# Attention's value products for two heads at once, in two 64-column tiles of TensorE's array

## The chip, the cores and the metric

One core of one Trainium2 chip runs the whole program. The metric is the device time of one execution in microseconds (us); the time of a kernel is the median over its runs. Engines are called as the profile calls them: PE (TensorE's matrix products), PEld (its weight loads), DVE (VectorE), ACT (ScalarE), POOL (GpSimd) and SP (SyncE, here a queue that issues DMAs).

## The reference, cut to what matters

The model has two layers, a Fourier layer and an attention layer, on 256 tokens and 256 context tokens. The change is in the attention of layer two: 64 query heads of width 64 share 8 heads of keys and values, and the softmax has one more term, the sink.

```python
s = jnp.einsum('bqhgd,bkhd->bhgqk', q, k).astype(jnp.float32) * (ATTN_HEAD_DIM ** -0.5)
if mask is not None:
    s = jnp.where(mask, s, NEG_INF)
sk = jnp.broadcast_to(sink..., s.shape[:-1] + (1,))
p = jax.nn.softmax(jnp.concatenate([s, sk], axis=-1), axis=-1)[..., :-1]
return jnp.einsum('bhgqk,bkhd->bqhgd', p.astype(v.dtype), v)      # the value products
...
y = jnp.moveaxis(o, 0, 1).reshape(b, n, D_BRANCH) * jax.nn.silu(z)
```

The last line shows what follows: the 64 x 64 = 4096 columns of attention output are multiplied by a gate computed from z, another product of the input with weights, and go through the output projection.

## The kernel before, in words

**Precision.** Operands are split in two parts, high and low, and a product is a sum of products of parts. Large products use three (high x high, high x low, low x high): that is `mm3`, lines 145 to 147, which nearly every group of the profile carries. For the value products both operands are f16 parts. The values v of a block of 128 keys are one tile `va` of 128 x 8 x 128: for each of the 8 value heads 64 columns of high parts and, beside them, 64 columns of low parts (lines 1248 to 1255; `v01[kb]` for the four blocks kb of 128 keys).

**The attention stage** is the loop over i from 0 to 65 (line 1550). Round i computes the scores and the softmax of head i (`stage_s`), and the value products of head i - 2 (`stage_o`), so that the work between lies two rounds apart. Between them stand two calls of `filler()`, each of which emits one unit of the large products of this layer from a fixed list (line 1379): q for the next heads, z for the blocks, and at the end the first part of the output projection. These units are what PE does while a head's softmax goes through DVE, ACT and a DMA. The order of the instructions on each engine is fixed when the program is built: a scheduler sorts what the loop emits by estimated readiness.

**One head's chain.** PE forms the scores of two blocks of 128 queries (lines 1483, 1484); DVE adds the mask and finds the maximum (1485); ACT takes the exponential (1488); DVE and ACT form the reciprocal of the sum; ACT and DVE write the normalised probabilities as a high and a low f16 half, `f` (1500, 1501); two DMAs on SP's queue transpose them into `ft`, keys on the partitions (1503). For heads 61 to 63 PE does the transposing (`stage_t`, lines 1506 to 1511). `ft` holds 8 x 2 x 128 columns: index j is 0 to 3 for the high parts of the four key blocks and 4 to 7 for the low parts. `ft` has 3 buffers.

**The value products before** (`stage_o`, line 1513). For each of the four key blocks two matmuls: the stationary operand is all 128 columns of `va` (64 high, 64 low), the moving operand is 256 queries of `ft`, once the high and once the low part. So 8 matmuls of 128x256 fill one PSUM tile `oo`, whose upper 64 rows hold the products with v's high part and the lower 64 rows those with its low part. ACT copies the lower half out (`ot`, 1524) and DVE adds it to the upper (`ob`, 1525); the head with odd number fills the lower half of `ob`. When both heads of a block are there, `emit_y` (1460) multiplies `ob` by the scale and by the gate `th`, if the unit of z for this block is done; else the unit of z calls it.

**PSUM.** All products share one pool of 8 banks (`psum()`, line 44).

**Another place that uses part of the array.** Early in the kernel `ada_tile` (line 279) has a stationary operand of only 32 columns. It writes four products into the four 32-row parts of one PSUM bank, `oa[0][j * 32 : (j + 1) * 32]`, which puts each of them in another 32-column tile of the array (line 286). The prediction uses its rows.

Of the kernel before, what the change touches and what calls it, by code (L numbers as in the profile page):

```python
# [10 lines left out]
F32 = mybir.dt.float32  # L11
F32R = mybir.dt.float32r
F16 = mybir.dt.float16
AF = mybir.ActivationFunctionType
ALU = mybir.AluOpType
AX = mybir.AxisListType

P = 128
# [4 lines left out]
N = 256  # L23
# [9 lines left out]
def tile_dit(ctx: ExitStack, tc: tile.TileContext, a: dict, out: bass.AP):  # L33
    nc = tc.nc
    V, S, PE, GP = nc.vector, nc.scalar, nc.tensor, nc.gpsimd
# [8 lines left out]
    def psum():  # L44
        return pp.tile([P, 512], F32, tag="ps", name="ps")
# [593 lines left out]
    for g in range(G):  # L639
        for j in {13: (8, 9), 14: (10, 11)}.get(g, (g - 5,) if 5 <= g < 13 else ()):  # L640
            t = up.tile([P, 1024], F32, name="pz", tag="pz", bufs=1)
# [217 lines left out]
    with tc.tile_pool(name="yp", reuse_waits="tile", bufs=32) as ypool:  # L859
# [171 lines left out]
        for i in range(32):  # L1031
# [26 lines left out]
            if kg >= 12:  # L1058
                for k in range(sw * 8 + (kg - 12) * 2, sw * 8 + (kg - 12) * 2 + 2):
                    t = act()  # L1060
# [79 lines left out]
    with tc.tile_pool(name="h1", reuse_waits="tile", bufs=16) as h1p:  # L1140
# [119 lines left out]
        with tc.tile_pool(name="at", reuse_waits="tile", bufs=2) as at:  # L1260
# [209 lines left out]
            def stage_s(i):  # L1470
                hk, blk, hh = i // 8, i // 2, i % 2
                p2, pr = (blk % 4) // 2, blk % 2
                kkh, kkl = kk[hk]
                q2 = qq[hk, p2][hh]
                pt = [at.tile([P, 512], F32, tag="p", name="p", bufs=3) for _ in range(2)]
                mx = at.tile([P, 2], F32, tag="mx", name="mx")
                sm = at.tile([P, 2], F32, tag="sm", name="sm")
                es = at.tile([P, 2], F32, tag="es", name="es")
                so = []
                for tb in range(2):  # L1480
                    o = psum()
                    st = q2[:, (pr * 2 + tb) * P : (pr * 2 + tb + 1) * P]
                    PE.matmul(o, st, kkh, start=True, stop=False)  # L1483
                    PE.matmul(o, st, kkl, start=False, stop=True)  # L1484
                    V.tensor_tensor_reduce(o, o, mask[:, tb, :], -0.125, nsink[:, i : i + 1], ALU.add, ALU.min, mx[:, tb : tb + 1])  # L1485
                    so.append(o)
                for tb in range(2):
                    S.activation(pt[tb], so[tb], AF.Exp, bias=mx[:, tb : tb + 1], scale=-1.0, accum_out=sm[:, tb : tb + 1])  # L1488
                S.activation(es, mx, AF.Exp, bias=sink[:, i : i + 1])
                V.scalar_tensor_tensor(sm, sm, 1.0 / PS, es, op0=ALU.mult, op1=ALU.add)  # L1490
                V.reciprocal(sm, sm)
                ft = at.tile([P, 8, 2, P], F16, tag="ft", name="ft", bufs=3)
                fs = []
                for tb in range(2):
                    if i < 61:
                        f = at.tile([P, 1024], F16, tag="f", name="f", bufs=3)
                    else:
                        f = actp.tile([P, 1024], F16, tag="act", name="f")
                        fs.append(f)
                    fa = S.activation(f[:, 0:512], pt[tb], AF.Copy, scale=sm[:, tb : tb + 1]).ins  # L1500
                    f_last[:] = fa, V.scalar_tensor_tensor(f[:, 512:1024], pt[tb], sm[:, tb : tb + 1], f[:, 0:512], op0=ALU.mult, op1=ALU.subtract).ins  # L1501
                    if i < 61:
                        nc.sync.dma_start_transpose(ft[:, :, tb, :], f)
                return ft, fs
# [5 lines left out]
                        PE.transpose(o[:, j, :], fs[tb][:, j * P : (j + 1) * P], ident16[0])  # L1510
                    (S.copy if tb == 0 else V.tensor_copy)(ft[:, :, tb, :], o)

            def stage_o(i, ft, fs):
                hk, blk, hh = i // 8, i // 2, i % 2
                oo = psum()
                for kb in range(4):
                    fh, fl = (ft[:, j, :, :].rearrange("p t q -> p (t q)") for j in (kb, 4 + kb))
                    PE.matmul(oo[:, 0:N], v01[kb][:, hk, :], fh, start=kb == 0, stop=False)  # L1518
                    PE.matmul(oo[:, 0:N], v01[kb][:, hk, :], fl, start=False, stop=kb == 3)  # L1519
                if hh == 0:  # L1520
                    obs[blk, 0] = at.tile([P, N], F32, tag="ob", name="ob", bufs=4)
                ob = obs[blk, 0]
                t = at.tile([64, N], F32, tag="ot", name="ot", bufs=1)
                S.copy(t, oo[64:128, 0:N])
                V.tensor_tensor(ob[hh * 64 : hh * 64 + 64, :], oo[0:64, 0:N], t, op=ALU.add)
                if hh == 1:
                    obs[blk, 1] = ob
                    emit_y(blk)

            first = 10  # L1530
            for i in range(first):
# [18 lines left out]
            for i in range(66):  # L1550
                if i % 8 == 0:
                    while defer:
                        defer.pop(0)[1]()
                if i == 61:
                    t = actp.tile([P, 1024], F16, tag="act", name="ident16")
                    ident16.append(t[:, 0:P])
                    S.copy(ident16[0], ident)
                y_sums(12, i if i < 60 else 99)
                if i == 62:
                    out_scale()  # L1560
                if i < 64:
                    pts[i] = stage_s(i)
                if i - 2 >= 61:
                    stage_t(*pts[i - 2])
                filler()
                if i >= 2:
                    stage_o(i - 2, *pts.pop(i - 2))
                filler()


# [244 lines left out]
```

## Time and profile before

| | us |
|---|---|
| median of 3 runs | 1761.97 |
| lowest and highest run | 1761.92, 1764.43 |
| span of the profiled execution, first to last instruction | 1759.3 |
| median less span, taken as what lies around the span | 2.67 |
| attention loop's value products, first and last start | 1139.2, 1617.5 |
| PE busy / DVE busy / ACT busy in the span | 1726.3 / 1404.7 / 1141.0 |

The page has no time of the profiled execution other than its span, so the difference to the median stands for the rest. A row of the timeline gives the start, the duration, the engine, the line, the operation, what it writes and reads, the array's part in use (128*128 is all of it, 128*32 is 32 of its columns), the shape and the number of merged instructions. A matmul's duration includes the way through the array, so matmuls that follow each other overlap in the list: what a matmul costs PE is the distance to the next start, not its duration. In brackets stands the idle time before an instruction and what ended it.

### The profile page before, as it was taken

The numbers are of one execution on the slowest core, as the hardware profiler recorded it, in microseconds if no ns is written. First come the engines' busy times: TensorE is split into PE (matmuls) and PEld (weight loads), VectorE is DVE, ScalarE is ACT, GpSimd is POOL, SyncE is SP. The second block draws the span as 40 slices with busy tenths as digits, with TensorE's granted clock in tenths as the row PEclk, the third lists the DMA queues.
The fourth block names the chain that finished last, engine by engine and source line by source line (L and its number), as shares of the span: only waits on it lengthen the run. The fifth ranks groups of instructions, "written<-read, shape, count | busy, mean of one in ns | idle before, by whom it ended". The sixth has DMA issues, their size and how long they took to land.

```text
span 1759.3 us, 27829 instructions
## 1 busy us (share of the span) xinstructions
PE 1726.3 (98%) x10051; PEld 1173.5 (67%) x10051; DVE 1404.7 (80%) x2443; ACT 1141.0 (65%) x2165; POOL 355.5 (20%) x485
## 2 busy tenths in 40 slices
PE   6999999999999999999999999999999999999997
PEld 4679999644444444446444745789889888987464
DVE  5779889797676786877689685989998889988755
ACT  5545556486777755465235496678888788888643
POOL 0002111211222104212310221412303221251001
PEclk9999999999999999999999999999999999999999
DMA  9998999778998969977997594588878888878643
GB/s 393 417 357 254 277 270 262 286 286 305 337 314 297 315 228 371 382 250 258 391 330 234 193 364 163 186 198 209 222 209 193 213 216 210 215 182 289 223 169 120
DMA packets 232298, 465.72 MB, mean 265 GB/s; under 512 B 154496, under 2 KB 154896, under 8 KB 205280
## 3 DMA queue, kind: packets, MB, share of 16 engines
q1 hardware_dynamic: 180672, 331.41, 57.4%
q0 software_dynamic: 47344, 125.58, 22.4%
q10 hardware_dynamic: 4144, 6.95, 1.1%
q8 instruction: 79, 1.29, 0.3%
q14 instruction: 59, 0.48, 0.1%
HBM read 419.30 MB, written 12.59 MB: 245 GB/s over the span
## 4 chain that ended last, share of the span: by engine, by line
PE 91%; DVE 3%; DMA 3%; ACT 2%; issue 1%; POOL 0%; ACTq 0%; POOLq 0%; SPq 0%; DVEq 0%
PE ps L145 27%; PE ps L146 27%; PE ps L147 27%; DMA raw<-in_awp 2%; PE ps L1518 2%; PE ps L1483 2%; PE ps L1484 2%; PE ps L1519 2%; PE ps L286 1%; ACT wf L137 1%; DMA ft<-f 0%; ACT act L877 0%; PE ps L1370 0%; DVE wf L138 0%; DVE act L984 0%
## 5 line engine op out<-in xcount | busy, mean ns | idle before, releaser
L67 DVE TENSOR_TENSOR wl<-raw,wh 128x1024 fp32r<-128x1024 f32 x152 | 200.2, 1321 | 44.3 <-ACT wh L66 30.6
L66 ACT CAST wh<-raw 128x1024 fp32r<-128x1024 f32 x152 | 158.7, 1045 | 62.9 <-PE ps L146 42.1
L146 PE MATMUL ps<-act,wf 128*128 128x512 f16 x512 | 194.0, 379 | 0.0
L147 PE MATMUL ps<-act,wf 128*128 128x512 f16 x512 | 191.1, 379 | 0.0
L145 PE MATMUL ps<-act,wf 128*128 128x512 f16 x512 | 189.8, 379 | 0.6 <-ACT wf L137 0.3
L145 PE MATMUL ps<-y,wf 128*128 128x512 f16 x448 | 169.8, 379 | 0.8 <-ACT wf L137 0.8
L146 PE MATMUL ps<-y,wf 128*128 128x512 f16 x448 | 169.8, 379 | 0.0
L147 PEld LDWEIGHTS <-wf 128*128 128x128 f16 x960 | 93.9, 98 | 113.2
L145 PEld LDWEIGHTS <-wf 128*128 128x128 f16 x960 | 93.7, 98 | 113.3 <-ACT wf L137 4.2
L146 PEld LDWEIGHTS <-wf 128*128 128x128 f16 x960 | 93.9, 98 | 109.0
L147 PE MATMUL ps<-y,wf 128*128 128x512 f16 x448 | 164.9, 379 | 0.0
L137 ACT ACTIVATE wf<-raw,nrm 128x1024 f16<-128x1024 f32 x56 | 63.5, 1147 | 131.1 <-PE ps L147 74.6
L145 PE MATMUL ps<-h,wh 128*128 128x256 f32 x512 | 145.5, 284 | 0.0
L147 PE MATMUL ps<-h,wl 128*128 128x256 f32 x512 | 142.9, 279 | 0.0
L146 PE MATMUL ps<-h,wh 128*128 128x256 f32 x512 | 142.9, 279 | 0.0
L138 DVE SCALAR_TENSOR_TENSOR wf<-raw,tn,wf 128x1024 f16<-128x1024 f32 x64 | 79.8, 1282 | 42.7 <-ACT wf L137 42.6
L829 ACT ACTIVATE act<-act 128x512 f32<-128x512 f32 x178 | 109.6, 618 | 6.2 <-DMA act<-in_wo 4.5
L1488 ACT ACTIVATE p<-ps,mx 128x512 f32<-128x512 f32 x128 | 87.9, 687 | 36.2 <-DVE mx L1485 34.2
L790 POOL DMA_DIRECT2D wa<-in_adw x64 | 34.2, 535 | 370.6 <-PE ps L147 142.5
L1501 DVE SCALAR_TENSOR_TENSOR f<-p,sm,f 128x512 f16<-128x512 f32 x128 | 102.2, 823 | 7.9 <-ACT f L1500 7.2
L1500 ACT ACTIVATE f<-p,sm 128x512 f16<-128x512 f32 x128 | 86.8, 718 | 25.3 <-issue 8.8
L146 PE MATMUL ps<-wl,h 128*128 128x512 f32 x256 | 101.3, 396 | 0.0
(430 smaller groups left out, 5021.8 us busy)
## 6 DMA issues: line engine op xcount, KB each, us to landing
raw<-in_wz SPq DMA_DIRECT2D x64, 1024.0 KB, 5.5
raw<-in_awp SPq DMA_DIRECT2D x32, 1024.0 KB, 12.7
zr<-in_adw SPq DMA_DIRECT2D x64, 512.0 KB, 6.9
wa<-in_adw POOLq DMA_DIRECT2D x64, 512.0 KB, 6.7
act<-in_wo POOLq DMA_DIRECT2D x128, 256.0 KB, 7.4
raw<-in_wo SPq DMA_DIRECT2D x32, 1024.0 KB, 8.2
raw<-in_wq SPq DMA_DIRECT2D x32, 1024.0 KB, 5.1
raw<-in_wu SPq DMA_DIRECT2D x32, 1016.0 KB, 6.0
```

Source lines behind the costliest of these rows:

```text
L66: last_cast[0] = S.copy(h, src).ins
L67: last_sub[0] = eng.tensor_tensor(l, src, h.bitcast(F32), op=ALU.subtract).ins
L137: last_cast[0] = S.activation(w[:, 0], src, AF.Copy, scale=up).ins
L138: last_sub[0] = V.scalar_tensor_tensor(w[:, 1], src, up, w[:, 0], op0=ALU.mult, op1=ALU.subtract).ins
L145: PE.matmul(o, wh, xh, start=start, stop=False)
L146: PE.matmul(o, wh, xl, start=False, stop=False)
L147: return PE.matmul(o, wl, xh, start=False, stop=stop).ins
L829: S.activation(t, t, AF.Square, accum_out=c)
L1483: PE.matmul(o, st, kkh, start=True, stop=False)
L1488: S.activation(pt[tb], so[tb], AF.Exp, bias=mx[:, tb : tb + 1], scale=-1.0, accum_out=sm[:, tb : tb + 1])
L1500: fa = S.activation(f[:, 0:512], pt[tb], AF.Copy, scale=sm[:, tb : tb + 1]).ins
L1501: f_last[:] = fa, V.scalar_tensor_tensor(f[:, 512:1024], pt[tb], sm[:, tb : tb + 1], f[:, 0:512], op0=ALU.mult, op1=ALU.subtract).ins
```

## The change

Two heads with even and odd number, which share value head and block, are computed together, in every second round. Each head gets a stationary operand of 64 columns: the even head writes rows 0 to 63 of the PSUM tile and so sits in the array's columns 0 to 63, the odd head writes rows 64 to 127 and sits in columns 64 to 127. For each key block there are three steps instead of two matmuls per head: high v with high p, low v with high p, high v with low p. (Before, the product of the two low parts was computed as well; it is left out now.) Twelve steps of two matmuls each stand for sixteen matmuls of full width. The sum over parts is made in PSUM, so that the copy by ACT and the addition by DVE are gone, and with them the tiles `ob` and `ot`; `emit_y` reads the PSUM tile itself. `ft` has 4 buffers instead of 3.

```diff
-                ft = at.tile([P, 8, 2, P], F16, tag="ft", name="ft", bufs=3)
+                ft = at.tile([P, 8, 2, P], F16, tag="ft", name="ft", bufs=4)
...
-            def stage_o(i, ft, fs):
-                hk, blk, hh = i // 8, i // 2, i % 2
-                oo = psum()
-                for kb in range(4):
-                    fh, fl = (ft[:, j, :, :].rearrange("p t q -> p (t q)") for j in (kb, 4 + kb))
-                    PE.matmul(oo[:, 0:N], v01[kb][:, hk, :], fh, start=kb == 0, stop=False)
-                    PE.matmul(oo[:, 0:N], v01[kb][:, hk, :], fl, start=False, stop=kb == 3)
-                if hh == 0:
-                    obs[blk, 0] = at.tile([P, N], F32, tag="ob", name="ob", bufs=4)
-                ob = obs[blk, 0]
-                t = at.tile([64, N], F32, tag="ot", name="ot", bufs=1)
-                S.copy(t, oo[64:128, 0:N])
-                V.tensor_tensor(ob[hh * 64 : hh * 64 + 64, :], oo[0:64, 0:N], t, op=ALU.add)
-                if hh == 1:
-                    obs[blk, 1] = ob
-                    emit_y(blk)
+            def stage_o(i, pair):
+                hk, blk = i // 8, i // 2
+                oo = psum()[:, 0:N]
+                steps = [(kb, c, j) for kb in range(4) for c, j in ((0, kb), (64, kb), (0, 4 + kb))]
+                for n, (kb, c, j) in enumerate(steps):
+                    for hh, ft in enumerate(pair):
+                        PE.matmul(oo[hh * 64 : hh * 64 + 64, :], v01[kb][:, hk, c : c + 64], ft[:, j, :, :].rearrange("p t q -> p (t q)"), start=n == 0, stop=n == len(steps) - 1)
+                obs[blk, 1] = oo
+                emit_y(blk)
...
-                if i >= 2:
-                    stage_o(i - 2, *pts.pop(i - 2))
+                if i >= 2 and i % 2:
+                    stage_o(i - 2, [pts.pop(j)[0] for j in (i - 3, i - 2)])
```

**PE, a head in the middle of the stage, before.** A unit of q or z (lines 145 to 147) is cut open and the 8 matmuls of one head, numbered ft_12949 here, are put in; each loads 128 columns of v and writes 128 rows.

```order
L145 MATMUL ps_13188<-h1_10424,wh_13126 128x256
L146 MATMUL ps_13188<-h1_10424,wh_13126 128x256
L147 MATMUL ps_13188<-h1_10424,wl_13127 128x256
L1518 LDWEIGHTS v_10818
L1518 MATMUL ps_13213<-ft_12949,v_10818 128x256
L1519 LDWEIGHTS v_10818
L1519 MATMUL ps_13213<-ft_12949,v_10818 128x256
L1518 LDWEIGHTS v_10822
```

The same place in the changed kernel: the head ft_12949 now waits for its partner ft_13049, and their matmuls of 64 rows alternate.

```order
L146 MATMUL ps_13280<-wl_13216,h1_10258 128x512
L147 MATMUL ps_13280<-wh_13215,h1_10258 128x512
L1519 LDWEIGHTS v_10818
L1519 MATMUL ps_13293<-ft_12949,v_10818 64x256
L1519 LDWEIGHTS v_10818
L1519 MATMUL ps_13293<-ft_13049,v_10818 64x256
L1519 LDWEIGHTS v_10818
L1519 MATMUL ps_13293<-ft_12949,v_10818 64x256
```

Over the program 64 blocks of 8 matmuls (512) became 32 pairs of 24 (768); 25 of the pairs stand in one piece.

**PE, the first heads of the stage, before.** The products of head 0 (ft_11116) come right behind a unit of q.

```order
L146 MATMUL ps_11045<-wl_11248,h1_10656 128x512
L147 MATMUL ps_11045<-wh_11247,h1_10656 128x512
L1518 LDWEIGHTS v_10818
L1518 MATMUL ps_11263<-ft_11116,v_10818 128x256
L1519 LDWEIGHTS v_10818
L1519 MATMUL ps_11263<-ft_11116,v_10818 128x256
```

In the changed kernel head 0 comes 28 matmuls of other lines later, with a single matmul of the pair inside a unit of z; the other 23 follow after 49 more, when head 1 (ft_11177) is due.

```order
L147 MATMUL ps_11334<-h1_10424,wl_11266 128x256
L1519 LDWEIGHTS v_10818
L1519 MATMUL ps_11359<-ft_11116,v_10818 64x256
L145 MATMUL ps_11334<-h1_10429,wh_11330 128x256
L146 MATMUL ps_11334<-h1_10429,wh_11330 128x256
```

```order
L147 MATMUL ps_11450<-h1_10419,wh_11386 128x256
L1519 LDWEIGHTS v_10818
L1519 MATMUL ps_11359<-ft_11177,v_10818 64x256
L1519 LDWEIGHTS v_10818
L1519 MATMUL ps_11359<-ft_11116,v_10818 64x256
```

Seven pairs are cut in this way, a single matmul ahead and 23 behind: the first four (heads 0 to 7) and the last three (heads 58 to 63).

**DVE, one block in the middle of the stage.** Before, the addition for a head (ob, line 1525) stands in the queue between the steps of other heads, and emit_y reads ob.

```order
L1525 TENSOR_TENSOR ob_12996<-ps_13111,ot_13120 64x256
L1501 SCALAR_TENSOR_TENSOR f_13063<-p_13044,sm_13047,f_13063 128x512
L1501 SCALAR_TENSOR_TENSOR f_13067<-p_13045,sm_13047,f_13067 128x512
L1485 ISA ps_13162,mx_13159<-ps_13162,mask_9991,nsink_9995 128x512
L1485 ISA mx_13159 128x1
L1466 SCALAR_TENSOR_TENSOR act_12929<-ob_12996,dsc_10001,th_13030 128x256
```

Now no addition is left, and emit_y reads the PSUM tile.

```order
L67 TENSOR_TENSOR wl_12990<-raw_12987,wh_12989 128x1024
L1454 SCALAR_TENSOR_TENSOR th_12926<-th_12926,ps_12846 128x256
L1490 SCALAR_TENSOR_TENSOR sm_12934<-sm_12934,es_12935 128x2
L1466 SCALAR_TENSOR_TENSOR act_12929<-ps_12871,dsc_10001,th_12926 128x256
L1491 RECIPROCAL sm_12934<-sm_12934 128x2
```

In SP's queue the 122 transposing DMAs and the weight loads keep their number; one load of z's weights near the start stands behind the transposes of one more head. POOL's queue is unchanged.

## The prediction, made before the changed kernel ran

> **What bounds the kernel now.** I read the page first (busy shares and the chain), then the table of windows over the attention stage, the groups of the stage by line and shape, the timeline around one head's products, and the waits of PE.
>
> ```profile
> span 1759.3 us, 27829 instructions
> PE 1726.3 (98%) x10051; PEld 1173.5 (67%) x10051; DVE 1404.7 (80%) x2443; ACT 1141.0 (65%) x2165; POOL 355.5 (20%) x485
> ...
> PE 91%; DVE 3%; DMA 3%; ACT 2%; issue 1%; POOL 0%; ACTq 0%; POOLq 0%; SPq 0%; DVEq 0%
> ...
> 1150.00:1200.00 50.00, 48.66 (x306) 42.17 (x305) 43.89 (x88) 39.51 (x77) 2.65 (x2) 1.00 0.81 208
> 1300.00:1350.00 50.00, 50.00 (x333) 44.31 (x332) 45.59 (x85) 40.54 (x79) 10.69 (x8) 1.00 0.80 217
> ```
>
> PE is busy 98% of the span and is 91% of the chain that ended last. In the middle of the stage (1300 to 1350; the columns are PE, PEld, DVE, ACT, POOL, granted clock, DMA share) PE has not a gap in 50 us, at full clock; DVE has 4.4 us free, ACT 9.5. So there a PE slot saved is a slot off the end, and work taken from ACT and DVE buys nothing. Only where PE waits do the others count, and those places are few:
>
> ```profile
> PE ps L1518 <- DMA ft<-f: 2.6, 2, 2.0
> PE ps L1518 <- ACT wh L66: 1.3, 1, 1.3
> ```
>
> **What the old products cost.** The timeline of PE around one head:
>
> ```profile
> 1303.68 0.40 PE L147 MATMUL ps<-wh,h 128*128 128x512 f32 x1
> 1303.92 0.28 PE L1518 MATMUL ps<-ft,v 128*128 128x256 f16 x1
> 1304.04 0.27 PE L1519 MATMUL ps<-ft,v 128*128 128x256 f16 x1
> ...
> 1304.70 0.27 PE L1519 MATMUL ps<-ft,v 128*128 128x256 f16 x1
> 1304.73 0.48 PE L145 MATMUL ps<-wh,h 128*128 128x512 f32 x1
> 1305.04 0.39 PE L146 MATMUL ps<-wl,h 128*128 128x512 f32 x1
> 1305.27 0.39 PE L147 MATMUL ps<-wh,h 128*128 128x512 f32 x1
> ```
>
> What counts is the distance of starts. Six steps from 1304.04 to 1304.70 make 0.110 us for a 128x256 f16 matmul. A 128x512 step is 0.23 (1305.04 to 1305.27), say 0.233. From 1303.68 to 1305.04 there are 1.36 us with two such steps and eight value matmuls in them: 1.36 - 0.466 = 0.894 for a head, 0.112 a matmul. So going from the f32 stream to f16 and back costs next to nothing (0.894 - 8 x 0.110 = 0.014). Two heads are 1.79 us.
>
> **What the new products cost.** Column tiles run in this kernel already: the products of 32 columns at line 286. One group, as PE's timeline and then (of a like group) the weight loads show it:
>
> ```profile
> 59.96 0.28 PE L147 MATMUL ps<-act,wpl 128*127 128x260 f32 x1
> 60.17 1.92 PE L286 MATMUL ps<-raw,c 128*32 128x512 f32 x16
> 62.03 0.38 PE L145 MATMUL ps<-act,wmh 128*127 128x256 f32 x1
> 62.25 0.28 PE L146 MATMUL ps<-act,wmh 128*127 128x256 f32 x1
> ```
>
> ```profile
> 42.00 0.16 PEld L286 LDWEIGHTS ps<-raw,c 128*32 128x32 f32 x8 [0.17 <-issue]
> 42.46 0.13 PEld L286 LDWEIGHTS ps<-raw,c 128*32 128x32 f32 x4 [0.30 <-issue]
> 42.89 0.13 PEld L286 LDWEIGHTS ps<-raw,c 128*32 128x32 f32 x4 [0.30 <-issue]
> ```
>
> ```profile
> L286 PEld LDWEIGHTS ps<-raw,c x256: 106/109/110, 18.7 to 115.3; 128*32 128x32 f32 x128
> L286 PE MATMUL ps<-raw,c x256: 589/592/617, 18.7 to 115.7; 128*32 128x512 f32 x128
> ```
>
> Sixteen matmuls with a median record of 0.592 take 1.92 together, so they run four at a time, in four rounds, and the loads come in fours 0.43 apart (42.46, 42.89): that is a round. Four loads of 0.109 lie within 0.13, so the loads of different tiles overlap, and eight of them are done 0.16 after the first, when only the first round runs: the next weights are loaded under the running matmuls. So two tiles side by side should make a step of two 64-column matmuls in the time of one old matmul, 0.110. Above it stands what two loads and two matmuls cost to issue; the fastest pairs of a load and a matmul are the transposes of the last heads:
>
> ```profile
> 1595.33 1.07 PE L1510 MATMUL ps<-ident,f 128*128 128x128 f16 x16
> L1510 PE MATMUL ps<-ident,f 128*128 128x128 f16 x48 | 3.2, 219 | 0.0
> ```
>
> (1.07 - 0.219) / 15 = 0.057 a pair, so 0.113 for two. I take 0.110, of the same shape and type, and keep 0.113 as the near bound.
>
> The group also shows a price that the old form doesn't have. From the start at 59.96 to the second normal start at 62.25 are 2.29 us; two normal steps of 0.117 (half the 0.233 of twice the columns) and four rounds of 0.43 are 1.95. The other 0.34 us, say 0.35 for the rounding, is the change from the full array to tiles and back: the stream stops before the first tile's matmul and again before the first full one, whose record is 0.38 for 0.28. A 64-column load is longer than a 32-column one; between 0.109 and the 0.188 of the 128 columns below I estimate 0.135, so 0.025 more, and take 0.375 us for each run of tile matmuls. Nothing hides it: PE is the bound.
>
> ```profile
> L145 PEld LDWEIGHTS ps<-h,wh 128*128 128x128 f32 x512 | 96.3, 188 | 1.7
> ```
>
> A pair is then 12 x 0.110 + 0.375 = 1.695 against 1.79: 0.095 saved, from four slots of 0.110 less one switch. The seven pairs that the new order cuts in two pay the switch twice and half a step more: 0.375 + 0.11 = 0.485 each.
>
> **The sum.** (1) 30 pairs from head 4 on: 30 x 0.095 = -2.85. (2) Five of the seven cut pairs are among them: 5 x 0.485 = +2.4. (3) The start, heads 0 to 3, where PE waits:
>
> ```profile
> 1136.79 0.40 PE L147 MATMUL ps<-wh,h 128*128 128x512 f32 x1
> 1139.22 0.27 PE L1518 MATMUL ps<-ft,v 128*128 128x256 f16 x1 [2.04 <-DMA ft<-f]
> ...
> 1162.30 0.28 PE L146 MATMUL ps<-h,wh 128*128 128x256 f32 x1
> 1163.92 0.27 PE L1518 MATMUL ps<-ft,v 128*128 128x256 f16 x1 [1.34 <-ACT wh L66]
> ```
>
> ```profile
> 1155.29 4.78 SPq L1503 DMA_TRANSPOSE ft<-f  x2
> ```
>
> ```profile
> 1150.00:1160.00 10.00, 10.00 (x85) 9.70 (x84) 9.57 (x23) 8.16 (x17) 0.00 (x0) 1.00 0.77 208
> ```
>
> Head 0's wait at 1139.22 goes, since head 0 is asked for 28 matmuls later. But PE then comes sooner to the second wait, for head 3, whose transposes are issued at 1155.29. That chain runs through DVE, 9.57 of 10 us busy, and doesn't move because PE is early. DVE loses three additions of 0.414 ahead of it, so head 3 lands 1.2 earlier at most; and there 23 matmuls are left to do (1.695) where 8 were (0.894). Net -1.2 + 0.8 = -0.4; the bounds are -2.2 (the whole first wait) and +0.8 (DVE's relief not felt). (4) A late wait, for head 60:
>
> ```profile
> 1591.19 0.40 PE L147 MATMUL ps<-wh,ys 128*128 128x512 f32 x1
> 1592.13 0.28 PE L1518 MATMUL ps<-ft,v 128*128 128x256 f16 x1 [0.55 <-DMA ft<-f]
> ```
>
> 0.94 less a step of 0.233 is 0.7; head 60 now waits for head 61 one round later, so it goes: -0.7.
>
> Together -2.85 + 2.4 - 0.4 - 0.7 = -1.55: the span goes from 1759.3 to 1757.75. The median lies 2.67 above this execution's span, so 1760.4.
>
> **What I cost at nothing.**
>
> ```profile
> L1525 DVE TENSOR_TENSOR ob<-ps,ot 64x256 f32<-64x256 f32 x64 | 26.5, 414 | 1.0
> L1524 ACT COPY ot<-ps 64x256 f32<-64x256 f32 x64 | 23.8, 371 | 3.9 <-PE ps L1519 2.2
> L1466 DVE SCALAR_TENSOR_TENSOR act<-ob,dsc,th 128x256 f32<-128x256 f32 x32 | 15.8, 495 | 0.2
> L1454 DVE SCALAR_TENSOR_TENSOR th<-th,ps 128x256 f32<-128x256 f32 x32 | 13.2, 413 | 0.0
> ```
>
> DVE's 26.5 and ACT's 23.8 us: PE covers both. emit_y reading PSUM: the same form from PSUM (L1454) is no longer, 0.413. A PSUM bank that is held until z is done, in the 8 first blocks of a value head, for half a unit of z (24 steps of 0.117, 2.8 us): the other seven banks cover it, and a pair takes one bank where it took two; uncovered, at most 8 x 2.8 = 22 us, which I don't expect as no row shows PE waiting for a bank. The weight load on SP that stands behind one head's transposes: PE has no row that waits for a weight load in this stage; if it did, about 1 us, once.
>
> **The rivals.**
>
> *The loads set the step (slower).* In four 32-column tiles the loads hide; two of 64 columns have twice the width each, and there are two every 0.110 us in f16 where the rows have four every 0.43. The step decides: the saving of (1), with (2) to (4) unchanged, gives no gain at 12 x step = 1.375, a step of 0.115, and a loss of 3.5 us at 0.124. If the two loads go one after the other, each exposes 0.135 less the 0.07 by which a load of 0.188 overlaps its neighbour in a stream of 0.117 steps: 0.13 a step, a pair of 1.935, 30 x 0.145 = +4.35, together +5.65: 1767.6. For it: two loads a step is a rate that no row shows. Against it: the eight loads within 0.16. Chance 0.22.
>
> ```profile
> L1518 PEld LDWEIGHTS <-v 128*128 128x128 f16 x256 | 24.9, 97 | 16.4 <-issue 11.7 <-DMA ft<-f 1.0 <-DVE wf L138 0.3
> ```
>
> A rule of the Trainium skill is for it: TensorEngine Tiling (Array Packing), "Gotcha 2", has column tiling and the fast weight load exclude each other. That the old f16 loads had a fast way to lose, the rows bear out, 0.097 here against 0.188 in f32 for the same 128 columns; what a 64-column f16 load takes without it no row shows. By the rule with the loads in turn the sum is this rival's 1767.6, with the loads side by side it stays 1760.4.
>
> *No load under a running tile.* Worse in kind: each step is then 0.110 + 0.135, a pair 3.3, 32 x 1.5 = +48: 1810. The second row of loads (42.46, while the round begun before it runs until about 42.86) speaks against it. Chance 0.02. The Trainium skill's TensorE: Matmul & The Clock Gate, "The mechanism", would lead here: a load overlaps running matmuls only if it goes to other rows of the array, and the two tiles share all rows. The trace doesn't agree, by that row.
>
> *The tiles don't run side by side,* so that the change doesn't do what it says: 24 x 0.110 + 0.375 = 3.0 a pair, 32 x 1.2 = +39: 1801. Against it stands the 1.92 us for sixteen records of 0.592. Chance 0.02.
>
> *The switch is cheaper (faster).* The 0.35 comes from f32 matmuls of 512 columns; f16 ones may leave the array sooner. At 0.2 a pair is 1.52: 30 x -0.27 = -8.1, the five cuts +1.55, the waits -1.1: -7.65, so 1754.3. At 0.32 the gain passes 3.5 us. For it: the old f16 run goes in and out for 0.014. Against it: a part of the 0.35 is the exposed load of the full array behind the tiles, 0.1 by the record of 0.38 for 0.28, and that load is the same here. Chance 0.26.
>
> **How the numbers follow.** About 0.2%, 3.5 us, is what a measurement of this kernel can tell from no change. The forecast, within that, has 0.48 and 1760.4. Faster is the cheap switch, with a start that keeps the whole first wait: 0.26. Slower is the three rivals with a dearer step: 0.22 + 0.02 + 0.02 = 0.26. The range goes from the cheap switch, 1754.3, to loads one after the other, 1767.6; beyond are the two rivals of 0.02 and the tails of the other two, under 0.2.
>
> **What would show it.** In the profile after: distances of 0.110 between matmuls of the same tile; a first full-array matmul behind each run with a record 0.1 longer than its neighbours', and 0.375 us more than the steps explain from the last full start to the second one behind; no wait at the first value product, and a longer one at head 3's; lines 1524 and 1525 gone and PE still at 50.00 of 50 us. Wrong would be: steps of 0.12 or more, a switch under 0.3, or PE waiting for DVE with a PSUM bank.

## The result, and the profile after

The changed kernel takes 1757.38 us (median of 17 executions, 1755.73 to 1763.98) against 1761.5 for the kernel before on the same chip: 0.9978 of it, interval 0.9971 to 0.9985, so 4.1 us or 0.22% less (2.6 to 5.1 us by the interval). A second series of the same kernel (first experiment) gave 0.9974, 0.9964 to 0.9983. The gain is real and 2.6 to 3 times what was predicted; its median lies just beyond the 3.5 us that were set as the bound, which both intervals include. The first profiled execution of it was disturbed (it was 5 us late before attention began), so the rows of "after" come from the second series' profile, of the same code.

The page's head and chain, and the two windows over the attention stage:

```profile
span 1755.1 us, 28142 instructions
PE 1724.2 (98%) x10307; PEld 1168.0 (67%) x10307; DVE 1393.7 (79%) x2379; ACT 1119.3 (64%) x2101; POOL 360.5 (21%) x485
...
PE 91%; DVE 4%; DMA 3%; ACT 1%; issue 1%; POOL 0%; ACTq 0%; POOLq 0%; SPq 0%; DVEq 0%
```

```profile
1150.00:1200.00 50.00, 48.10 (x315) 40.34 (x314) 43.34 (x81) 38.40 (x74) 3.25 (x2) 1.00 0.90 209
1300.00:1350.00 50.00, 50.00 (x367) 44.66 (x366) 44.27 (x77) 39.21 (x76) 11.13 (x8) 1.00 0.87 211
```

The span is 4.2 us shorter than before's 1759.3. PE is as full as it was: all of 1300 to 1350, at full clock. The copies and additions taken off ACT and DVE were 50 us before (23.8 and 26.5), though by the page their busy times are only 21.7 and 11.0 us shorter; PE's share of the chain is the same 91%. So the place to look for the gain is the length of PE's own stream. PE's timeline around one pair, and the weight loads of that pair:

```profile
1308.34 0.40 PE L147 MATMUL ps<-wh,h 128*128 128x512 f32 x1
1308.67 1.50 PE L1519 MATMUL ps<-ft,v 128*64 128x256 f16 x24
1310.10 0.50 PE L145 MATMUL ps<-wh,h 128*128 128x512 f32 x1
1310.44 0.40 PE L146 MATMUL ps<-wl,h 128*128 128x512 f32 x1
```

```profile
1308.67 1.23 PEld L1519 LDWEIGHTS <-v 128*64 128x64 f16 x24 [0.37 <-issue]
```

As in the prediction, what counts is the distance of starts. From 1308.34 to 1310.44 are 2.10 us, less two normal steps of 0.233: about 1.63 for the pair. Over the 20 pairs in one piece whose neighbours are full matmuls the median is 1.623 (1.613 to 1.633), where two heads took 1.79 before and 1.695 was forecast. The 24 loads are done (1309.90) 0.27 us before the run's last matmuls are (1310.17).

Where a pair is cut, its first matmul stands alone, and it shows what going to the tiles and back costs:

```profile
1140.50 0.28 PE L147 MATMUL ps<-h,wl 128*128 128x256 f32 x1
1140.71 0.30 PE L1519 MATMUL ps<-ft,v 128*64 128x256 f16 x1
1140.93 0.38 PE L145 MATMUL ps<-h,wh 128*128 128x256 f32 x1
1141.16 0.28 PE L146 MATMUL ps<-h,wh 128*128 128x256 f32 x1
```

From 1140.50 to 1141.16 are 0.66, less two steps of 0.117: 0.426 for one matmul (0.413 to 0.433 in the five of the seven whose neighbours are single rows, median 0.423). If a step is 0.110, the switch is 0.31, and 0.31 + 12 x 0.110 = 1.63 gives the pair too. The rows above say where the 0.31 lies: 0.10 ahead of the first tile matmul (1308.67 where 1308.57 was due), 0.11 behind the last (1.43 from 1308.67 to 1310.10, less 12 x 0.110), and 0.10 in the first full matmul, whose record is 0.50 for 0.40.

Two of before's waits at the first heads have become one, for head 3, and it is longer (1.90 for 1.34; the view put the 1.34 down to ACT's L66, the prediction took it for head 3's transposes):

```profile
1163.10 1.50 PE L1519 MATMUL ps<-ft,v 128*64 128x256 f16 x23 [1.90 <-DMA ft<-f]
```

The late one, for head 60, is gone; the whole program's waits of PE hold no other of this line:

```profile
PE ps L1519 <- DMA ft<-f: 1.9, 1, 1.9
```

And emit_y from PSUM is no longer than from SBUF (0.495 before):

```profile
L1519 PEld LDWEIGHTS <-v 128*64 128x64 f16 x768 | 40.2, 110 | 12.0 <-issue 8.5 <-DMA ft<-f 2.1
L1466 DVE SCALAR_TENSOR_TENSOR act<-ps,dsc,th 128x256 f32<-128x256 f32 x32 | 15.3, 479 | 1.3 <-PE ps L1519 0.9
```

### The profile page after: what moved, and what is told of

Read it like the earlier page. It is cut to its first block, busy times and chain, and to the rows that moved or that the text cites. A ratio compares the mean times of both kernels' runs of the same rounds, so it can differ in the third digit from the quotient of the medians.

```text
span 1762.1 us, 28142 instructions
## 1 busy us (share of the span) xinstructions
PE 1730.3 (98%) x10307; PEld 1174.1 (67%) x10307; DVE 1395.5 (79%) x2379; ACT 1118.5 (63%) x2101; POOL 360.9 (20%) x485
## 4 chain that ended last, share of the span: by engine, by line
PE 76%; DVE 3%; ACT 1%; DMA 1%; issue 1%; POOL 0%; POOLq 0%; ACTq 0%; DVEq 0%
PE ps L145 23%; PE ps L146 23%; PE ps L147 23%; PE ps L1519 3%; PE ps L1484 2%; PE ps L1483 2%; ACT act L877 0%; DMA ft<-f 0%; ACT wf L137 0%; DVE wl L67 0%; DVE wf L138 0%; DVE act L878 0%; DMA sink<-in_sink 0%; PE ps L1370 0%; PE ps L997 0%
## 5 line engine op out<-in xcount | busy, mean ns | idle before, releaser
L67 DVE TENSOR_TENSOR wl<-raw,wh 128x1024 fp32r<-128x1024 f32 x152 | 211.5, 1393 | 54.9 <-ACT wh L66 44.9
L66 ACT CAST wh<-raw 128x1024 fp32r<-128x1024 f32 x152 | 158.9, 1046 | 90.2 <-PE ps L146 73.0
L137 ACT ACTIVATE wf<-raw,nrm 128x1024 f16<-128x1024 f32 x56 | 63.4, 1145 | 133.6 <-PE ps L147 73.7
L1500 ACT ACTIVATE f<-p,sm 128x512 f16<-128x512 f32 x128 | 88.3, 717 | 36.2 <-DMA ft<-f 26.5
L147 PE MATMUL ps<-wh,h 128*128 128x512 f32 x256 | 101.1, 396 | 0.0
```

Of the source, the lines that this page charges most:

```text
L66: last_cast[0] = S.copy(h, src).ins
L67: last_sub[0] = eng.tensor_tensor(l, src, h.bitcast(F32), op=ALU.subtract).ins
L137: last_cast[0] = S.activation(w[:, 0], src, AF.Copy, scale=up).ins
L147: return PE.matmul(o, wl, xh, start=False, stop=stop).ins
```

## The experiments

My theory after the result: PE's stream sets the time; a run of tile matmuls costs a fixed 0.31 us and 0.110 for each step (a step is one matmul of each tile, side by side), and that fixed part was forecast too dear. The rivals: the gain comes from the work taken off ACT and DVE after all, or from the start of the stage. The times are medians; "over" and "under" compare with after's second series unless another is named.

**The change again**, to see how large the gain is.

> The changed kernel itself, once more, because its first profiled execution had a clock of 0.994 and lay 5 us behind the old kernel's before the attention stage began. Switch theory (each run of tile matmuls costs PE 0.31 us beyond its steps of 0.11, 39 runs, and the old two heads 1.786 a pair): 1757 to 1758 against 1761.5 before, ratio 0.9975 to 0.9985, and a span near 1755.5 with the same 1.63 us a pair. Relief theory (the gain is that ACT and DVE lost 24 and 26 us): the same time, so this run only gives the base of the others.

1757.03 (1756.08 to 1758.85), 0.9974 of before, with seven single matmuls (39 runs of tile matmuls for 32 pairs). The gain is there again.

**The odd head first.** In a pair, the head that comes later is asked for first, so nothing of the pair can be issued early and no pair is cut.

```
-                    for hh, ft in enumerate(pair):
+                    for hh, ft in ((1, pair[1]), (0, pair[0])):
```

> In each step the odd head's matmul stands before the even head's, so that the first matmul of a pair waits for the head that comes last and no pair is cut in two (32 runs of 24, none of 1). Switch theory: the five cuts in places where PE never waits go, 5 x 0.425 = 2.1 us, and the two at the start give 0 to 0.8: 2 to 3 us under the changed kernel, so near 1755. Relief theory: ACT and DVE do the same work, so no change within 0.5 us, or slower at the start, where PE can't begin a pair early.

1756.31 (0.9971, 0.996 to 0.9982): 0.7 under, with intervals that overlap, where 2 to 3 were expected; the span is 1.8 under. All 32 runs are whole and still 1.623. What the seven cuts gave, 7 x 0.42 = 3.0, was partly paid back at the start: PE now waits for head 1 at the first pair, longer than it had waited for head 3.

```profile
1146.68 1.50 PE L1519 MATMUL ps<-ft,v 128*64 128x256 f16 x24 [2.75 <-DMA ft<-f]
```

**Four heads in a run.** With the odd head first, two pairs are put behind each other every fourth round (`for k in (i - 2, i - 4)`, then emit_y for both; five ft buffers, two each of qa and qb to make room). Sixteen switches less, nothing else of PE's.

> Two pairs in one run: the products of four heads every fourth round, 16 runs of 48 tile matmuls instead of 32 of 24 (odd head first, later pair first; ft has 5 buffers, qa and qb 2 instead of 3 to make room). Switch theory: 16 switches less, 16 x 0.31 = 5.0 us under the run with the odd head first, near 1750, if the longer way of a head makes no new wait at the start or at the end. Relief theory: no change, or slower by the waits for the fourth head. New waits at the start of the stage (the first run needs head 3) of up to 3 us would hide a part: then 1751 to 1753.

1755.75 (0.9968, 0.9959 to 0.9978), 0.6 under the odd-first kernel and short of what was expected; the span is 1.8 under. PE's timeline around one of the 16 runs:

```profile
1193.86 0.40 PE L147 MATMUL ps<-wh,h 128*128 128x512 f32 x1
1194.19 2.81 PE L1519 MATMUL ps<-ft,v 128*64 128x256 f16 x48
1196.93 0.50 PE L1483 MATMUL ps<-kkh,qa 128*128 128x512 f32 x1
1197.27 0.40 PE L1484 MATMUL ps<-kkl,qa 128*128 128x512 f32 x1
```

3.41 from 1193.86 to 1197.27 less 0.467: 2.943 for 24 steps. With 1.623 for 12 and 0.423 for one, these lie on a line: (2.943 - 1.623) / 12 = 0.110 and (1.623 - 0.423) / 11 = 0.109 a step, 0.31 a run. The time fell by less than 16 x 0.303 = 4.8. Part of the rest is in waits for the first and the third run's heads, since four have to be there at once (the odd-first kernel had one wait, of 2.8), and PE waits 1.0 for DVE's L67 near the stage's end; 4.8 less these 2.6 is 2.2, near the 1.8 by which the spans differ:

```profile
PE ps L1519 <- DMA ft<-f: 4.4, 2, 2.7
```

**One head behind the other.** The loops are exchanged, 12 matmuls of the even head and then 12 of the odd.

```
-                for n, (kb, c, j) in enumerate(steps):
-                    for hh, ft in enumerate(pair):
+                for hh, ft in enumerate(pair):
+                    for n, (kb, c, j) in enumerate(steps):
```

> The changed kernel's 24 matmuls of a pair in another order: twelve of the even head, then twelve of the odd one, so that each matmul follows one of the same tile. Side by side theory (two tiles run at once and only at the joint can they overlap): 24 steps of 0.11 less one, 2.9 us a pair for 1.62, 32 x 1.3 = 41 us more than the changed kernel, near 1798. If a tile matmul only took half the time of a full one, with no overlap: no change, 1757. If the weight loads of one tile can't hide under that tile's own matmul, the step is over 0.11 here, up to 0.22.

1787.82 (1.0147, 1.0131 to 1.0162), 30.8 over. Two runs of its PE timeline, a pair and, near the end, a head by itself:

```profile
1304.82 0.39 PE L147 MATMUL ps<-wh,h 128*128 128x512 f32 x1
1305.14 2.40 PE L1519 MATMUL ps<-ft,v 128*64 128x256 f16 x24
1307.47 0.50 PE L145 MATMUL ps<-wh,h 128*128 128x512 f32 x1
1307.81 0.40 PE L146 MATMUL ps<-wl,h 128*128 128x512 f32 x1
...
1607.30 0.40 PE L147 MATMUL ps<-wh,ys 128*128 128x512 f32 x1
1607.63 1.50 PE L1519 MATMUL ps<-ft,v 128*64 128x256 f16 x12
1609.05 0.50 PE L145 MATMUL ps<-wh,ys 128*128 128x512 f32 x1
1609.39 0.39 PE L146 MATMUL ps<-wl,ys 128*128 128x512 f32 x1
```

12 matmuls of one head alone take 2.09 - 0.467 = 1.623, exactly what 24 alternating ones take: so in the changed kernel the second head costs nothing, and the tiles do run side by side. As the step stays at 0.110 with one tile alone, its loads hide under that tile's own matmuls too. The pair in series takes 2.523, 0.90 more and not the 1.32 (12 x 0.110) that I had expected. I read the missing 0.42, about four steps, as the second tile's start beside the first one's end; the merged row doesn't show it.

**A run cut by one full matmul, and the control.** Both with the odd head first; one unread 128x256 f16 matmul on the whole array goes into the middle of each run (`if n == 6: PE.matmul(spare, ...)`), or in the control behind its end.

> Odd heads first, and in the middle of each block's run (after 6 of its 12 pairs) one matmul on the whole array into a bank that nobody reads, so that the array is switched from tiles to whole and back once more per block, 32 times. The switch theory (0.31 us for every run of tiles, 0.11 us for a step, both read from runs of 1, 12 and 24 steps): 32 x (0.31 + 0.11) = 13.4 us over the odd-first kernel's 1756.3, 1769.7. Rival, the fixed 0.31 belongs to the block (its first read of the turned heads, or the output bank) and not to the switch: 32 x 0.11 = 3.5 us, 1759.8. Waits at the start of the stage can swallow 1 us of either.

> The control: the same unread matmul on the whole array, at the end of each block's run, where the array goes back to whole anyway. Both theories: 32 x 0.11 = 3.5 us over the odd-first kernel's 1756.3, 1759.8; the runs of 24 tile matmuls stay at 1.62 us.

Cut: 1766.66 (1.0024, 1.0014 to 1.0034). Behind: 1756.66 (0.9971, 0.9959 to 0.9982). The difference is 10.0 us for 32 cuts, 0.31 each (10.3 by the two spans). The timeline of PE, of the cut run (the tile matmuls are L1521 there, the full one L1519) and then of the control (L1519, and L1520 the full one):

```profile
1313.09 0.39 PE L147 MATMUL ps<-wh,h 128*128 128x512 f32 x1
1313.40 0.85 PE L1521 MATMUL ps<-ft,v 128*64 128x256 f16 x12
1314.18 0.28 PE L1519 MATMUL ps<-ft,v 128*128 128x256 f16 x1
1314.39 0.85 PE L1521 MATMUL ps<-ft,v 128*64 128x256 f16 x12
1315.17 0.50 PE L145 MATMUL ps<-wh,h 128*128 128x512 f32 x1
1315.51 0.40 PE L146 MATMUL ps<-wl,h 128*128 128x512 f32 x1
```

```profile
1309.28 0.39 PE L147 MATMUL ps<-wh,h 128*128 128x512 f32 x1
1309.59 1.50 PE L1519 MATMUL ps<-ft,v 128*64 128x256 f16 x24
1311.03 0.28 PE L1520 MATMUL ps<-ft,v 128*128 128x256 f16 x1
1311.07 0.47 PE L145 MATMUL ps<-wh,h 128*128 128x512 f32 x1
1311.38 0.39 PE L146 MATMUL ps<-wl,h 128*128 128x512 f32 x1
```

2.42 - 0.467 = 1.953 (median 1.963) against 2.10 - 0.467 = 1.633: the cut costs 0.33. The price belongs to the switch and not to the block, for which the rival gave 3.5 us. My expectation of 13.4 and 3.5 over the odd-first kernel (10.4 and 0.4 measured) was too high in both. Behind the run the full matmul is nearly free, 0.01 to 0.02 and not 0.11: the price of a run's end is a stall that a short matmul can fill. What fits is that the next full weights, 0.20 by PEld's record, begin to load at 1311.03, with that matmul. In the cut run it needn't be free: the rows have it 0.12 late, and the next tile matmul 0.21 behind it, which is its own 0.11 and 0.10 for the way to the tiles. By that reading this switch costs 0.22, without the 0.10 that the first f32 matmul behind a run pays; no run here separates the two.

**The copies and additions put back**, to see whether taking them off ACT and DVE was worth nothing, as the prediction had it. Odd head first, and for each head a copy and an addition of the old shape from the new PSUM tile, unread:

```
+                for hh in range(2):
+                    ob = at.tile([64, N], F32, tag="ob", name="ob", bufs=1)
+                    t = at.tile([64, N], F32, tag="ot", name="ot", bufs=1)
+                    S.copy(t, oo[64:128, :])
+                    V.tensor_tensor(ob, oo[0:64, :], t, op=ALU.add)
```

> Odd head first as in the run before, and behind each pair two copies by ACT and two additions by DVE of the old shapes, whose result nobody reads: ACT and DVE get their 24 and 26 us back, PE's work is that of the run before. Switch theory: PE has no gap in the stage, so at most 1 us over the run with the odd head first, from the start of the stage. Relief theory: the gain over the old kernel is lost in whole or large part, 1759 to 1761.

1774.96 (1.0082, 1.0069 to 1.0094): 18.6 over the odd-first kernel, and a clear miss. The longest waits of PE between 1200 and 1600, where the odd-first kernel has none, and one of ACT's:

```profile
PE ps L146 <- DVE wl L67: 5.7, 6, 2.8
PE ps L147 <- DVE wl L67: 2.5, 6, 0.4
```

```profile
ACT ot L1523 <- DVE ob L1524: 22.2, 20, 2.6
```

PE stood still for 10.5 of 400 us, mostly for DVE's half of the split of the weights (L67). ACT's second copy waits for DVE's first addition, 20 times, 22 us in all, and its queue stands behind it. My guess for the cause was the one buffer of ot.

**The same with two buffers of ot** and the additions in place.

> The run with the copies back was 18 us slower than the one without (1774.96 against 1756.3), and PE waited for DVE's halves of weights there, so the statement that ACT and DVE's work is covered by PE is in doubt. Here the same copies and additions, but each pair's two copies have a buffer of their own (ot has 2, the additions write over ot), so that ACT's second copy no longer waits for DVE's first addition. If the bunching did it (ACT, in order, stands in a chain of copy, addition, copy, addition while other work is queued behind): 1757 to 1763. If the amount of work on DVE and ACT did it (26 and 24 us): 1773 to 1776, as before.

1777.18 (1.0086, 1.0073 to 1.01). The guess fell; the wait is still there, and what it is for stays open:

```profile
ACT ot L1522 <- DVE ot L1523: 23.4, 22, 2.6
```

**The same number of copies and additions, from ft and the mask in SBUF**, with no chain from ACT to DVE.

> The same number of copies by ACT and additions by DVE, but they read the transposed probabilities in SBUF and the mask instead of the product's PSUM tile, and no addition needs a copy: nothing waits for PE, and no engine for the other. The result is read by nobody. If the amount of work did it: 1770 or more. If the waits in order (for PE's run to end, and of ACT and DVE for each other) did it: 1756 to 1760.

1792.95 (1.0172, 1.0158 to 1.0186), the slowest of all, though DVE was less busy than in the odd-first kernel (341 of the 400 us, against 357). This kernel tests nothing of what it was made for, because the additions and copies came to stand ahead of their transposes in the queues:

```profile
DVE ob L1524 <- DMA ft<-f: 43.0, 23, 3.8
```

It lost 36.6 us to the odd-first kernel, against 7.9 to 10.7 for the work alone below, so waits in the queues of ACT and DVE can cost more than the work there; how they reach PE stays open. PE's own waits were 14.6 us for POOL (at the turning of q, L1370) and 4.0 for DVE's L67.

**The work alone.** As the last, but both operations read only the mask, and each is held behind the newest head's last multiplication on its own engine (`tc.issue_after(f_last[0])`, `tc.issue_after(f_last[1])`), so that they wait for no other engine.

> Odd heads first, and for each head one copy of 64x256 on ACT and one addition of 64x256 on DVE, the number and size that the change removed, but reading only the mask in SBUF, each placed in its engine's queue behind that head's last multiplication: they wait for no other engine. They are left unread. Theory A (in the runs with the copies put back PE stood still because ACT and DVE wait in order for each other, not because they have no time left): within 4 us of the odd-first kernel's 1756.3, at most 1760. Theory B (ACT and DVE have no time to spare in this stage, whatever the copies wait for): 1770 or more, with PE idle before L145 to L147 and the releaser DVE or ACT, as in the runs with the copies back.

**The work alone, spread**: one copy and one addition in every round, not two of each in every second.

> The same dummy copy on ACT and dummy addition on DVE as in the run with the work alone, 64 of each, reading only the mask, each behind its head's last multiplication, but one of each in every round of the loop (as the kernel before spread its copies and additions) and not two together in every second round. Theory C (two together in every second round are what PE notices: DVE comes 0.9 us later to the next pieces of a weight): within 3 us of the odd-first kernel's 1756.3, and PE idle under 1 us between 1200 and 1600. Theory B (the amount of the work, wherever it stands): as with two together, 1767, PE idle some 6 us there for DVE and ACT.

1766.97 (1.0032, 1.0021 to 1.0044) and 1764.23 (1.0017, 1.0007 to 1.0027): 10.7 and 7.9 over the odd-first kernel, between what the theories said, in both. The longest wait of PE in the same stretch, with two of each together and then spread (PE's gaps there are 6.2 and 4.4 us in all; the first profile is of the longest of its nine executions, 1771.35):

```profile
PE ps L146 <- DVE wl L67: 3.8, 3, 3.1
```

```profile
PE ps L146 <- DVE wl L67: 2.5, 3, 1.8
```

So adding the bare work costs roughly half of the 18.6, and the other half comes with what its operands wait for. If anything that is too much for the work: the addition from two SBUF operands took 0.600 in the mean here, where the removed one, with an operand in PSUM, took 0.414 (the group in the spread kernel, between 1200 and 1600). That mean is of two kinds: 42 of them took 0.410, and 10 took 1.4, every one of these beside an instruction of POOL; of the removed ones none was long. A good part of the price lies in one place near the stage's end, in products of the output projection (`ys`): the longest waits, 3.09 and 1.79, end at 1587.58 and 1580.78, and the mean granted clock is 0.64 to 0.67 from 1585 to 1595 in the first and 0.66 from 1580 to 1585 in the second. With the copies put back PE has such a wait too (2.81, to 1591.57), but 16 others all through the stage besides.

```profile
L1567 DVE TENSOR_TENSOR ob<-mask 64x256 f32<-64x256 f32 x52 | 31.2, 600 | 0.0
```

**The best of both.** Pairs at the start and the end (i < 10, i > 61), where waits eat what a longer run saves, and four heads a run between; odd head first.

> The first eight heads and the last four in pairs, the others four heads to a run (13 runs less than in pairs alone). In the run with four heads throughout a merge took 0.303 us off each two pairs, but the first runs waited 2.7 and 1.8 us for their heads. If those waits at the start are what kept the gain down (1755.75 for an expected 1751): 13 x 0.30 = 3.9 us under the run in pairs, near 1752.5. If the runs of four delay other things in the middle of the stage: no better than 1755.75.

1753.18 (1752.17 to 1756.72), 0.9955 of before (0.9943 to 0.9968): 8.6 us under the kernel before and 3 to 4 under the changed one, the fastest here. With 19 runs for 32, 13 switches are gone, 13 x 0.30 = 3.9 by the measured price against 3.1 measured from the odd-first kernel's 1756.3. It waits for a head once, and for DVE's L67 once (1.3, at 1570.72); 1150 to 1200 has no gap, as in the odd-first kernel:

```profile
PE ps L1519 <- DMA ft<-f: 3.0, 1, 3.0
```

```profile
1150.00:1200.00 50.00, 50.00 (x342) 43.34 (x341) 43.40 (x85) 40.05 (x77) 3.21 (x2) 1.00 0.86 211
```

## Why the prediction was right, and where its sum was off

**The mechanism held.** PE set the time, the tiles ran side by side with a step of 0.110 (shown by 12 alone and 24 alternating both at 1.623), and each run paid once for going to the tiles and back (shown by the runs of 1, 12 and 24 steps and by the cut). The forecast of no measurable change rested on that price, and there the size was off. The time lies inside the range, but the two series together show a change, and by the medians it falls where the forecast had put its cheap-switch rival, with 0.26, and not within the 3.5 us that it gave 0.48.

**The mis-sized term: the switch, 0.375 forecast, 0.31 measured.** The 0.35 was read from runs of 32-column tiles in f32, and 0.025 was added for the wider load. Both parts were too much. The 64-column load's record is 0.110 and not 0.135, as short as the 32-column ones, so nothing was to be added; and the run itself leaves and enters faster by 0.04 than the 0.35 that was read (the row gave 0.34). Type, width and neighbours all differ between the two places, so which of them it is stays open. A difference of 0.065 is small, but a pair saves four steps less one switch, 0.16 for 0.095, and that 30 times. The forecast had named this as its "switch is cheaper" rival, with 0.32 as the point where the gain passes 3.5 us; at 0.31 the case lies just beyond it. The 0.2 at which that rival was priced, and its 1754.3, were too far.

**The sum, by its steps**, against the spans 1759.3 and 1755.1: (1) 30 pairs, -2.85 forecast, 30 x 0.163 = -4.9 measured. (2) Five cuts, +2.4 forecast, 5 x 0.42 = +2.1. (4) The late wait is gone, -0.7 as forecast. (3) The start is what is left of -4.2: -0.7, for -0.4 forecast; the first wait went and the one for head 3 grew to 1.90, as said. Counted from the rows it is -1.0: waits of 1.90 for 2.04 + 1.34, and two pairs with two cuts, 4.09, for four heads at 0.894, 3.58. With that the sum is -4.5, 0.3 more than the spans differ by.

**The rivals.** Loads that set the step: no; 24 loads take 1.23 us, 0.05 apart, and the step stays 0.110. The Trainium skill's TensorEngine Tiling (Array Packing), "Gotcha 2" (no fast weight load with column tiling), agrees with the load's record so far as it goes, 0.110 for 64 columns where 128 took 0.097 in one piece; but the longer load is hidden. No load under a running tile: no, by the same rows and by the step of one head alone. The rule in the Trainium skill's TensorE: Matmul & The Clock Gate, "The mechanism" (a load overlaps a running matmul only in other rows of the array), doesn't hold for these rows as it stands: both tiles use all rows, and loads 0.110 long fit into steps of 0.110 for two of them. That section's own exception, a load into the background weight buffer, no row here tells apart. Tiles one after the other: no, by the serial run.

**What was costed at nothing.** Emit_y from PSUM and the PSUM bank: no row shows a price (0.479 a step; no wait of PE for a bank). ACT's and DVE's freed 50 us: the sum above, with the start counted, closes to 0.3 us on PE's own terms and leaves nothing for them, and before's PE had no wait for either engine between 1200 and 1600. So taking them away bought nothing that shows, as forecast. But the reason given, that PE covers them, was too broad: put back into the new order, they cost 8 to 19 us. And the busy time, from which that reason was read, doesn't tell when PE is hit. The same stretch, 1200 to 1600, with the copies put back and then with the work spread:

```profile
1200.00:1600.00 400.00, 389.47 (x2783) 338.63 (x2781) 366.12 (x643) 317.97 (x638) 110.07 (x84) 1.00 0.85 202
1200.00:1600.00 400.00, 395.62 (x2835) 346.38 (x2835) 370.52 (x669) 321.60 (x654) 115.60 (x89) 1.00 0.85 208
```

DVE is busier in the second, and PE's gaps are 4.4 us for 10.5. Before had DVE busy for 362 and PE never waiting for it; the last kernel, with 359, waits 1.3. One reason is that busy time isn't a fixed amount of work: DVE lost 22.0 us of additions in this stretch, but its busy time only went from 362.4 to 357.3, in part because its split of the weights (L67) went from 1307 to 1393 ns in the mean, with the same median (1224 and 1225). More of them are long: of those listed singly 28 took over 1.4 us, where 17 had, and all of these lie beside an instruction of POOL, of the others fewer than one in five. So DVE's busy time holds time in which, it seems, POOL held it up; no run takes POOL away to show it. What sets the old order apart, in which the same copies cost nothing, isn't settled; that its copies came one head at a time is at most a part, since spreading them took back 2.7 of 10.7, within the intervals.

## What to carry to other kernels

Price a change to column tiles for each run: a fixed part for the switch (0.31 us here) and a step that two tiles share, so a few saved matmuls only pay in runs that stay whole; ask for the operand that comes last first, and join runs where their operands are there anyway (0.30 each). Read a fixed part from runs of different lengths, a single matmul among them, and don't carry it over from another type and width where the result hangs on hundredths. And "covered" holds for the order in which it was seen: work on a nearly full engine that is hidden in one order can hold up the bound engine in another.

## What the runs showed of the hardware that was not expected

Behind a long wait of PE the granted clock was at times half for a few microseconds, and not each time. In the control with one matmul behind, PE had waited 3.07 us at the first pair, and in the kernel that mixes pairs and fours 3.01 at the same place; their windows from 1145 to 1150, the control first:

```profile
1145.00:1150.00 5.00, 3.58 (x28) 3.04 (x29) 4.97 (x6) 2.38 (x5) 3.39 (x3) 0.66 0.79 236
```

```profile
1145.00:1150.00 5.00, 2.96 (x33) 2.62 (x34) 4.97 (x6) 2.05 (x5) 4.09 (x3) 1.00 0.85 262
```

The clock is 0.66 in the mean of one (0.50 from 1149.5 to 1150) and 1.00 in the other. In the slowed one the pair's run took 2.59 us for 1.50:

```profile
1146.41 2.59 PE L1519 MATMUL ps<-ft,v 128*64 128x256 f16 x24 [3.07 <-DMA ft<-f]
```

So a wait of 3 us can cost a microsecond or more beyond itself. Shorter ones can too: in the changed kernel's first profile the wait was 2.00, and the 23 matmuls behind it took 2.54. What decides between the two cases no run here shows.
